# Down projections of two of three feed-forward parts: four feature tiles of a part by seven half-width products

## The chip, the cores and the metric

The kernel runs on one core of a Trainium2 chip. The engines are TensorE (PE, matrix products into PSUM), VectorE (DVE), ScalarE (ACT), GpSimd (POOL) and the queue that issues most transfers (SP). A transfer is issued by a queue and carried by the core's DMA engines. Each engine works through its own instructions in order and waits on semaphores for the others. The metric is the device time of one execution in microseconds (us); of the kernel before there are three runs. A profile is one further execution, recorded by the hardware.

## The reference

Two layers, 512 positions, 1024 features. Each layer has two feed-forward blocks with a mixer (a convolution and a differential attention) between them:

```python
def swiglu(h, w_gate, w_up, w_down):
    return (jax.nn.silu(h @ w_gate) * (h @ w_up)) @ w_down
...
    for l in range(DEPTH):
        x = x + 0.5 * swiglu(rms_norm(x, ffn1_norm[l]), ffn1_w_gate[l], ffn1_w_up[l], ffn1_w_down[l])
...
        x = x + jnp.concatenate([conv_out, diff_out], axis=-1) @ w_out[l]
        x = x + 0.5 * swiglu(rms_norm(x, ffn2_norm[l]), ffn2_w_gate[l], ffn2_w_up[l], ffn2_w_down[l])
```

The gated width is 2816, that is 22 feature tiles of 128; the output has 8 tiles of 128 features. All of it is float32 with a tight tolerance.

## The kernel before

**Products.** A float32 product is made of three matmuls on split operands: high weight by high activation, high by low, low by high (mm3, L174 to L178). A weight chunk of 128 x 1024 is loaded into a tile wraw; ACT copies it, rounded, into whi (L100), and DVE subtracts to get wlo (L101). These tiles come from rings shared by tag: five wraw, four each of whi and wlo, two half-size ones each (wraw2, whi2, wlo2). A slot is given out again when the last reader of its tile has been put in order. The order on every engine is made at build time by a scheduler; keep_in_program_order pins the first matmul of a group.

**The feed-forward block (ffn, L416).** x is kept as [128, 8, 512], features by positions. The 22 tiles are done in three parts of 5, 8 and 9 (PARTS). A part first computes its gated tiles (gate and up, silu, product), then projects them down into all eight outputs and adds them to x (L486). So there are 4 blocks x 3 parts.

**Seven products for gate and up (seven, L369).** From the sixth tile on, gate and up of a tile are the two rows of a two-by-two block product: the 1024 input features are two halves, the 512 positions two halves of 256. Seven products of half blocks (Strassen's scheme in Winograd's form) stand for eight. The weight sums are made in sums (L130 to L158) by POOL and by one accumulating DMA (L152), the activation sums in Halves. The products accumulate in two PSUM banks, a and d in one, b and c in the other; parts of them are copied to a tile keep by ACT (L391, L395, L400) in between. The seventh product and what follows it (rest, L406) are put off into the next tile, by way of late and finish, so that they stand behind the next tile's first two products.

**The down projection (L475 to L488)** is plain: for each output m, one bank, and for each of the part's tiles three full-width matmuls of 512 columns, 3 x 8 x 8 = 192 in part two and 216 in part three. gather loads eight blocks of 128 x 128 at a time, in pieces where they do not lie together. finish runs before it. In part three, after(m) hands x[m] to the next norm (Prep.tile, L260): ACT scales (L262) and squares (L271), DVE makes the low half (L263), POOL adds up the squares (L275).

**Banks.** Pairs of PSUM banks are taken in rotation from three tags (sc, po, mm) by a running number; two more tags, tp and y, have one bank each. Each block and each mixer starts the rotation at a number of its own.

Of the kernel before, what the change touches and what calls it, by code (L numbers as in the profile page):

```python
# [11 lines left out]
F32 = mybir.dt.float32  # L12
F32R = mybir.dt.float32r
# [5 lines left out]
P = 128  # L19
DEPTH = 2  # L20
# [23 lines left out]

PARTS = ((0, 5), (5, 8), (13, 9))
PLAIN = PARTS[0][1]
# [21 lines left out]
def trunk(ctx: ExitStack, tc: tile.TileContext, xt, par, lamv, relb, onehot,  # L68
# [12 lines left out]
    def f32(ap):  # L81
        return ap.bitcast(F32)
# [285 lines left out]

    def seven(halves, w, banks, fp, before, last):  # L369

# [25 lines left out]
        go(b, "g2", "b21")  # L396
        if not last:
            go(c, "all", "b22")
        go(a, "g1u2u1", "t2")
        S.activation(keep[:, 2], a, AF.Copy)  # L400
        if last:
            go(c, "all", "b22")
        V.tensor_tensor(two, two, g, op=ALU.add)
# [11 lines left out]

    def ffn(pr, gu, dn, after, lead=None, aside=None):  # L416
        with tc.tile_pool(name="ffn", bufs=1) as fp:
            r = halves = None
            for m0, many in PARTS:
                hh, held, late = [], [], []  # L420

                def gated(n, us):
                    hi = fp.tile([P, SEQ], F32R, tag=f"hh{n}", name="hh")
                    lo = fp.tile([P, SEQ], F32R, tag=f"hl{n}", name="hl")
                    S.activation(hi, us, AF.Copy)
                    V.tensor_tensor(lo, us, f32(hi), op=ALU.subtract)
                    hh.append((hi, lo))

                def finish():
                    if late:  # L430
                        n, rest = late.pop()
                        gated(n, rest())

                for mm in range(many):
# [3 lines left out]
                    if m >= PLAIN:  # L438
                        w = sums(gu[m, 0], gu[m, 1])
                        late.append((mm, seven(halves, w, pair_banks(m), fp, finish, mm == many - 1)))  # L440
                        continue
                    if lead and m < 2:
                        w = lead[m]
                    else:

                        w = [(by_halves if lead and m == 2 else chunk)(gu[m, 0]), chunk(gu[m, 1])]
                    held.append((mm, w, pair_banks(m)))
                    if m == 0:
# [21 lines left out]
                    if not halves:  # L470
                        halves = Halves(fp, pr, r)
                finish()
                if m0 == 0:
# [4 lines left out]
                for m in range(KT):  # L478

                    ps = bank(turn_tag(m0 + many + m // 2), "ps_d")  # L480
                    for kk in range(many):
                        b = m * many + kk
                        if b % 8 == 0:
                            w = gather(dn, blocks[b : b + 8])
                        mm3(ps, wpart(w, b % 8), hh[kk], kk == 0, kk == many - 1)
                    V.scalar_tensor_tensor(x[:, m, :], ps, 0.5, x[:, m, :], op0=ALU.mult, op1=ALU.add)  # L486
                    if m0 + many == FT:
                        after(m)  # L488


# [55 lines left out]

    def mixer(l, pr, after):
        with tc.tile_pool(name="mix", bufs=1) as mp, tc.tile_pool(name="mt", bufs=2) as mt:
            us = [None] * CT
            row = {}  # L550
            turn = iter(range(12))
            held = []
# [307 lines left out]
    def aside():  # L860
        make_scalars()
        make_bias()

    for l in range(DEPTH):
        nxt = {}
# [10 lines left out]

        ffn(pr, gu1[l], dn1[l], then(l, "mix_norm"), *((lead, aside) if l == 0 else ()))
        mixer(l, nxt["p"], then(l, "ffn2_norm"))
        ffn(nxt["p"], gu2[l], dn2[l], then(l + 1, "ffn1_norm") if l + 1 < DEPTH else last)
        pr = nxt["p"]  # L880
# [74 lines left out]
```

## Time and profile before

| What | us |
|---|---|
| Median of 3 runs | 1791.35 |
| Lowest and highest run | 1789.62, 1792.2 |
| Span of the profiled execution, first to last instruction | 1789.9 |
| PE busy in it | 1780.6 |
| DVE, ACT, POOL busy in it | 1192.0, 893.1, 668.9 |

The page's rows of engine totals give busy time, its share of the span and the number of instructions. The slices give tenths of busy time in 40 equal stretches, and PEclk the clock that TensorE was granted. The chain of waits follows the work that ended last back from the end; in order of time it gives start, length and what it was, merged where equal instructions follow each other. A window lists start and end, then busy us of PE, PEld (weight loads, beside PE), DVE, ACT and POOL with their instruction counts, the clock, and the share and rate of DMA. A row of a group gives line, engine, operation, output <- inputs, shapes, count, then busy us and mean ns of one, then the idle time of the engine just before them and what ended it. Rows of the timeline give start and length in us. Matmuls overlap, so that the distance of their starts, not their mean length, is what one costs.

### The profile page before, as it was taken

The page shows a single profiled execution, that of the slowest core. Times are in us where ns is not written, and L with a number is a line of the kernel's source. Part 1 is how long each engine was busy: PE and PEld are TensorE (multiplying, and loading weights), DVE is VectorE, ACT ScalarE, POOL GpSimd, SP SyncE. Part 2 cuts the span into 40 slices and gives each one's busy share as a digit, 9 for nine tenths or more (in the row PEclk, how much of TensorE's full clock was granted, in tenths as well). Part 3 has the DMA queues.
Part 4 walks back from the last instruction along what each step waited for, and adds up shares of the span by engine and source line. Part 5 has one row for each costly group of instructions (what it writes and reads, how often), then busy time and mean ns, then how long its engine had stood idle before and what let it go on. Part 6 is the DMA issues. An engine that isn't in the chain of part 4 may idle for free.

```text
span 1789.9 us, 28369 instructions
## 1 busy us (share of the span) xinstructions
PE 1780.6 (99%) x10861; PEld 1592.3 (89%) x10861; DVE 1192.0 (67%) x1833; ACT 893.1 (50%) x1487; POOL 668.9 (37%) x469
## 2 busy tenths in 40 slices
PE   9999999999999999999999999999999999999999
PEld 7899899888788899899888998998887988998997
DVE  6866477558858767477576655765788487664872
ACT  6455265445845455255433643644558354552651
POOL 2243242269863132232202412412798431422420
PEclk9999999999999999999999999999999999999999
DMA  7376466323122367367324655663230233664651
GB/s 247 106 181 179 112 175 179 114 98 94 36 83 88 90 165 191 104 171 195 101 93 101 169 167 124 174 180 118 71 117 25 71 107 97 167 172 112 168 163 59
DMA packets 111721, 231.24 MB, mean 129 GB/s; under 512 B 12151, under 2 KB 33414, under 8 KB 111584
## 3 DMA queue, kind: packets, MB, share of 16 engines
q1 hardware_dynamic: 91488, 191.93, 33.4%
q0 software_dynamic: 19808, 37.33, 12.7%
q8 instruction: 85, 1.39, 0.3%
q14 instruction: 52, 0.43, 0.1%
q10 hardware_dynamic: 288, 0.16, 0.0%
HBM read 227.26 MB, written 3.42 MB: 129 GB/s over the span
## 4 chain that ended last, share of the span: by engine, by line
PE 97%; DVE 2%; DMA 0%; issue 0%; SPq 0%; ACT 0%; DVEq 0%
PE ps_pair L386 38%; PE ps_d L177 9%; PE ps_d L174 9%; PE ps_d L178 9%; PE ps_pair L178 5%; PE ps_pair L177 5%; PE ps_pair L174 5%; PE ps_sc L726 2%; PE ps_pair L604 2%; PE ps_pair L602 2%; PE ps_pair L603 2%; PE ps_out L174 1%; PE ps_out L177 1%; PE ps_out L178 1%; PE ps_o L756 1%; DVE actl L263 1%
## 5 line engine op out<-in xcount | busy, mean ns | idle before, releaser
L100 ACT ACTIVATE whi<-wraw 128x512 fp32r<-128x512 f32 (+2 forms) x600 | 466.1, 801 | 617.9 <-PE ps_pair L386 225.1
L101 DVE TENSOR_TENSOR wlo<-wraw,whi 128x512 fp32r<-128x512 f32 (+2 forms) x557 | 514.4, 946 | 225.2 <-ACT whi L100 220.4
L386 PE MATMUL ps_pair<-acth,wlo 128*128 128x256 f32 x1088 | 307.9, 283 | 0.0
L386 PE MATMUL ps_pair<-actl,whi 128*128 128x256 f32 x1088 | 307.9, 283 | 0.0
L386 PE MATMUL ps_pair<-acth,whi 128*128 128x256 f32 x1088 | 307.9, 283 | 0.0
L177 PE MATMUL ps_d<-hl,whi 128*128 128x512 f32 x704 | 274.0, 389 | 0.0
L178 PE MATMUL ps_d<-hh,wlo 128*128 128x512 f32 x704 | 272.9, 389 | 0.0
L174 PE MATMUL ps_d<-hh,whi 128*128 128x512 f32 x704 | 269.1, 389 | 0.0
L152 POOL DMA_DIRECT2D wraw<-in_gu x68 | 82.0, 1206 | 407.3 <-DMA wraw<-in_gu 188.8
L386 PE MATMUL ps_pair<-th,wlo 128*128 128x256 f32 x816 | 230.9, 283 | 0.0
L386 PE MATMUL ps_pair<-tl,whi 128*128 128x256 f32 x816 | 230.8, 283 | 0.0
L386 PE MATMUL ps_pair<-th,whi 128*128 128x256 f32 x816 | 230.8, 283 | 0.0
L157 POOL TENSOR_TENSOR wraw<-wraw 128x512 f32<-128x512 f32 x68 | 106.6, 1568 | 328.0 <-DMA wraw<-in_gu 252.5
L386 PEld LDWEIGHTS ps_pair<-acth,whi 128*128 128x128 f32 x1088 | 208.9, 192 | 0.3
L386 PEld LDWEIGHTS ps_pair<-actl,whi 128*128 128x128 f32 x1088 | 208.9, 192 | 0.3
L386 PEld LDWEIGHTS ps_pair<-acth,wlo 128*128 128x128 f32 x1088 | 208.9, 192 | 0.0
L486 DVE SCALAR_TENSOR_TENSOR x<-ps_d,x 128x512 f32<-128x512 f32 x96 | 64.8, 689 | 180.4 <-PE ps_d L178 180.1
L177 PE MATMUL ps_pair<-actl,whi 128*128 128x512 f32 x448 | 174.6, 391 | 0.3 <-DVE actl L263 0.2
L174 PE MATMUL ps_pair<-acth,whi 128*128 128x512 f32 x448 | 173.9, 392 | 0.7 <-ACT whi L100 0.7
L178 PE MATMUL ps_pair<-acth,wlo 128*128 128x512 f32 x448 | 174.3, 391 | 0.0
L386 PEld LDWEIGHTS ps_pair<-tl,whi 128*128 128x128 f32 x816 | 156.5, 192 | 0.7
L386 PEld LDWEIGHTS ps_pair<-th,whi 128*128 128x128 f32 x816 | 156.5, 192 | 0.6
(171 smaller groups left out, 3264.9 us busy)
## 6 DMA issues: line engine op xcount, KB each, us to landing
wraw<-in_gu SPq DMA_DIRECT2D x208, 256.0 KB, 4.0
wraw<-in_gu SPq DMA_DIRECT2D x104, 512.0 KB, 3.7
wraw<-in_gu POOLq DMA_DIRECT2D x68, 512.0 KB, 5.7
wraw<-in_wqkv SPq DMA_DIRECT2D x24, 512.0 KB, 3.6
wraw<-in_dn SPq DMA_DIRECT2D x84, 128.0 KB, 3.0
wraw<-in_dn SPq DMA_DIRECT2D x32, 256.0 KB, 3.3
wraw<-in_wag SPq DMA_DIRECT2D x16, 512.0 KB, 3.6
wraw<-in_wout SPq DMA_DIRECT2D x16, 512.0 KB, 3.6
```

Of the source, the lines that this page charges most:

```text
L100: S.activation(hi, raw, AF.Copy)
L101: low = (eng or V).tensor_tensor(out=lo, in0=raw, in1=f32(hi), op=ALU.subtract)
L152: nc.gpsimd.dma_start(two.rearrange("p (b c) -> p b c", b=2), u[:, h[0]].unsqueeze(1).broadcast_to([P, 2, 512]), accum_op=ALU.add)
L157: G.tensor_tensor(more[:, h[0]], two[:, h[1]], whole[:, h[0]], op=ALU.add)
L174: first = T.matmul(ps, wh, xh, start=start, stop=False)
L177: T.matmul(ps, wh, xl, start=False, stop=False)
L178: T.matmul(ps, wl, xh, start=False, stop=stop)
L386: mm = T.matmul(ps, l, r, start=first and i == j == 0, stop=False, skip_group_check=True)
L486: V.scalar_tensor_tensor(x[:, m, :], ps, 0.5, x[:, m, :], op0=ALU.mult, op1=ALU.add)
L602: T.matmul(ps[n], xh[:, t], wh, start=k == 0, stop=False)
L603: T.matmul(ps[n], xh[:, t], wl, start=False, stop=False)
L604: T.matmul(ps[n], xl[:, t], wh, start=False, stop=k == KT - 1)
```

## The change

PARTS gains a third number, the pairs of feature tiles that are projected by seven products: none in part one, two in parts two and three. There, four feature tiles of the part are the inner dimension (two halves, each made of two tiles: the even and the odd ones), two outputs A = 2q and B = 2q + 1 are the rows, and the two halves of the positions the columns. The part's other four or five tiles are projected plainly into the same two outputs, A into the banks of b and c, B into a spare bank (tp or y).

- down_sums loads the blocks of A and B (g and u), and POOL makes four sums of 256 columns from them; what does not fit (the ninth tile) goes with one sum into a tile "two". Then all are split into high and low.
- seven_down issues the products, evicts parts of the banks into keep with ACT, adds these to x with POOL (lines 501 and 510 of the new file) and the banks to x with DVE (lines 513, 516, 520). Its last product, with the last update of x[B], is put off into the next pair, or into the next part's first tile, as rest.
- Gated.add takes the place of gated: beside the high and low of a gated tile it makes, for the first four tiles of a part, sums of their half blocks, on ACT and DVE, and stores them split.
- The running number of the banks is passed on (turn) through parts and into the mixer.
- seven loses its argument last, by which the last tile of a part ordered two products otherwise; the last gated tile of a part is finished within the first pair of the down projection.

```diff
@@ -42,7 +42,7 @@
 HS = SEQ // 2
-PARTS = ((0, 5), (5, 8), (13, 9))
+PARTS = ((0, 5, 0), (5, 8, 2), (13, 9, 2))
 PLAIN = PARTS[0][1]
 SPACE = 392
-    def seven(halves, w, banks, fp, before, last):
+    def seven(halves, w, banks, fp, before):
...
-        if not last:
-            go(c, "all", "b22")
+        go(c, "all", "b22")
         go(a, "g1u2u1", "t2")
         S.activation(keep[:, 2], a, AF.Copy)
-        if last:
-            go(c, "all", "b22")
         V.tensor_tensor(two, two, g, op=ALU.add)
         S.activation(g, two, AF.Silu)
...
-    def ffn(pr, gu, dn, after, lead=None, aside=None):
+    def down_sums(dn, m0, many, pairs, q):
+        def pull(raw, at, m, k, end):
+            while k < end:
+                half, f = divmod(m0 + k, HALF)
+                b, w = m * HALF + f, 1
+                while (b + w) % 8 and k + w < end and f + w < HALF:
+                    w += 1
+                c = b % 8
+                nc.sync.dma_start(raw[:, at : at + w * P], dn[half, b // 8][:, c * P : (c + w) * P])
+                at, k = at + w * P, k + w
+        A, B = 2 * q, 2 * q + 1
+        whole, over, J = min(many, 8), max(many - 8, 0), pairs * P
+        u, two, g = ring("wraw"), ring("wraw2", 512), ring("wraw")
+        pull(u, 0, B, 0, whole)
+        pull(g, 0, A, 0, whole)
+        pull(two, J, A, whole, many)
+        pull(two, J + over * P, B, whole, many)
+        more = ring("wraw")
+        def odd_even(t):
+            t = t[:, : 2 * J].rearrange("p (j e c) -> p e j c", e=2, c=P)
+            return t[:, 0], t[:, 1]
+        def row(t, n):
+            return t[:, n * J : (n + 1) * J].rearrange("p (j c) -> p j c", c=P)
+        (u1, u2), (g1, g2) = odd_even(u), odd_even(g)
+        G.tensor_tensor(row(two, 0), u1, u2, op=ALU.add)
+        G.tensor_tensor(u1, u1, g1, op=ALU.add)
+        G.tensor_tensor(row(more, 0), row(two, 0), g1, op=ALU.add)
+        G.tensor_tensor(row(more, 1), row(more, 0), g2, op=ALU.add)
+        def split(raw, tag, n, width):
+            hi, lo = ring("whi" + tag, n), ring("wlo" + tag, n)
+            parts_of(raw[:, :width], hi[:, :width], lo[:, :width])
+            return lambda at: (hi[:, at * P : (at + 1) * P], lo[:, at * P : (at + 1) * P])
+        two = split(two, "2", 512, J + 2 * over * P)
+        u = split(u, "", 1024, whole * P)
+        g = split(g, "", 1024, whole * P)
+        more = split(more, "", 1024, 2 * J)
+        return {
+            "u2u1": two,
+            "u2": lambda j: u(2 * j + 1),
+            "g1u1": lambda j: u(2 * j),
+            "g1": lambda j: g(2 * j),
+            "g2": lambda j: g(2 * j + 1),
+            "g1u2u1": more,
+            "all": lambda j: more(pairs + j),
+            "A": lambda k: g(k) if k < 8 else two(pairs + k - 8),
+            "B": lambda k: u(k) if k < 8 else two(pairs + over + k - 8),
+        }
+    def seven_down(q, w, h, banks, spare, fp, before, pairs, many, after, last):
+        A, B = 2 * q, 2 * q + 1
+        a, d = banks[0][:, :HS], banks[0][:, HS:]
+        b, c = banks[1][:, :HS], banks[1][:, HS:]
+        keep = fp.tile([P, 4, HS], F32, tag="gn", name="keep", bufs=2)
+        def by_two(t):
+            return t.rearrange("p (n c) -> p n c", n=2)
+        def go(ps, wt, xt, first=False):
+            for j in range(pairs):
+                (wh, wl), (xh, xl) = w[wt](j), h.get(xt, j)
+                for i, (l, r) in enumerate(((wh, xh), (wh, xl), (wl, xh))):
+                    mm = T.matmul(ps, l, r, start=first and i == j == 0, stop=False, skip_group_check=True)
+                    if i == j == 0:
+                        tc.keep_in_program_order(mm)
+        def plain(ps, wt, first=False):
+            for k in range(2 * pairs, many):
+                (wh, wl), (xh, xl) = w[wt](k), h.hh[k]
+                for i, (l, r) in enumerate(((wh, xh), (wh, xl), (wl, xh))):
+                    start = first and i == 0 and k == 2 * pairs
+                    mm = T.matmul(ps, l, r, start=start, stop=False, skip_group_check=True)
+                    if i == 0 and k == 2 * pairs:
+                        tc.keep_in_program_order(mm)
+        go(c, "u2u1", "t1", first=True)
+        S.activation(keep[:, 3], c, AF.Copy, scale=0.5)
+        go(d, "u2", "t4", first=True)
+        before()
+        go(a, "g1", "b11")
+        S.activation(keep[:, :2], by_two(banks[0]), AF.Copy, scale=0.5)
+        G.tensor_tensor(by_two(x[:, B, :]), by_two(x[:, B, :]), keep[:, 1::2], op=ALU.subtract)
+        go(b, "g2", "b21")
+        if last:
+            plain(banks[1], "A")
+        else:
+            go(c, "all", "b22")
+            plain(banks[1], "A")
+        go(a, "g1u2u1", "t2")
+        S.activation(keep[:, 2], a, AF.Copy, scale=0.5)
+        G.tensor_tensor(by_two(x[:, A, :]), by_two(x[:, A, :]), keep[:, 0::2], op=ALU.add)
+        if last:
+            go(c, "all", "b22")
+        V.scalar_tensor_tensor(x[:, A, :], banks[1], 0.5, x[:, A, :], op0=ALU.mult, op1=ALU.add)
+        after(A)
+        plain(spare, "B", first=True)
+        V.scalar_tensor_tensor(x[:, B, :], spare, 0.5, x[:, B, :], op0=ALU.mult, op1=ALU.add)
+        def rest():
+            go(a, "g1u1", "t3")
+            V.scalar_tensor_tensor(
+                by_two(x[:, B, :]), a.unsqueeze(1).broadcast_to([P, 2, HS]), -0.5, by_two(x[:, B, :]),
+                op0=ALU.mult, op1=ALU.add,
+            )
+            after(B)
+        return rest
+    class Gated:
+        STORE = (("ht", "ht", "rb"), ("s0", "s1", "s2"))
+        def __init__(self, fp, pairs):
+            self.fp, self.pairs = fp, pairs
+            self.hh, self.sums = [], []
+        def part(self, tag):
+            pool, bufs = (act, None) if tag == "rb" else (self.fp, 2 if tag == "ht" else None)
+            return pool.tile([P, SEQ], F32R, tag=tag, name="hs", **({"bufs": bufs} if bufs else {}))
+        def add(self, n, us):
+            a, b = slice(0, HS), slice(HS, SEQ)
+            paired = n < 2 * self.pairs
+            if paired and n % 2 == 0:
+                self.hold = self.fp.tile([P, SEQ], F32, tag=("hh8", "hl8")[n // 2 % 2], name="hold")
+                S.activation(self.hold, us, AF.Copy)
+                V.tensor_tensor(us[:, b], self.hold[:, a], self.hold[:, b], op=ALU.subtract)
+            hi = self.fp.tile([P, SEQ], F32R, tag=f"hh{n}", name="hh")
+            lo = self.fp.tile([P, SEQ], F32R, tag=f"hl{n}", name="hl")
+            S.activation(hi, us, AF.Copy)
+            V.tensor_tensor(lo, us, f32(hi), op=ALU.subtract)
+            self.hh.append((hi, lo))
+            if not paired or n % 2 == 0:
+                return
+            t = self.hold
+            V.tensor_tensor(t[:, b], us[:, b], t[:, b], op=ALU.subtract)
+            V.scalar_tensor_tensor(t[:, a], t[:, a], -1.0, t[:, b], op0=ALU.mult, op1=ALU.subtract)
+            V.scalar_tensor_tensor(us[:, a], us[:, a], -1.0, t[:, a], op0=ALU.mult, op1=ALU.subtract)
+            hi, lo, four = (self.part(tag) for tag in self.STORE[n // 2])
+            S.activation(hi, t, AF.Copy)
+            V.tensor_tensor(lo, t, f32(hi), op=ALU.subtract)
+            S.activation(four[:, a], us[:, a], AF.Copy)
+            V.tensor_tensor(four[:, b], us[:, a], f32(four[:, a]), op=ALU.subtract)
+            self.sums.append((hi, lo, four))
+        def get(self, name, j):
+            a, b = slice(0, HS), slice(HS, SEQ)
+            if name == "t4":
+                return self.sums[j][2][:, a], self.sums[j][2][:, b]
+            hi, lo = self.sums[j][:2] if name in ("t2", "t3") else self.hh[2 * j + (name[0] == "b" and name[1] == "2")]
+            c = a if name in ("b11", "b21", "t2") else b
+            return hi[:, c], lo[:, c]
+    def ffn(pr, gu, dn, after, turn, lead=None, aside=None):
         with tc.tile_pool(name="ffn", bufs=1) as fp:
             r = halves = None
-            for m0, many in PARTS:
-                hh, held, late = [], [], []
-                def gated(n, us):
-                    hi = fp.tile([P, SEQ], F32R, tag=f"hh{n}", name="hh")
-                    lo = fp.tile([P, SEQ], F32R, tag=f"hl{n}", name="hl")
-                    S.activation(hi, us, AF.Copy)
-                    V.tensor_tensor(lo, us, f32(hi), op=ALU.subtract)
-                    hh.append((hi, lo))
-                def finish():
-                    if late:
-                        n, rest = late.pop()
-                        gated(n, rest())
+            late = []
+            def finish():
+                if late:
+                    late.pop()()
+            for m0, many, pairs in PARTS:
+                held, h = [], Gated(fp, pairs)
+                gated, hh = h.add, h.hh
                 for mm in range(many):
                     m = m0 + mm
...
                         w = sums(gu[m, 0], gu[m, 1])
-                        late.append((mm, seven(halves, w, pair_banks(m), fp, finish, mm == many - 1)))
+                        rest = seven(halves, w, pair_banks(turn + mm), fp, finish)
+                        late.append(lambda n=mm, rest=rest, gated=gated: gated(n, rest()))
                         continue
                     if lead and m < 2:
                         w = lead[m]
                     else:
+                    held.append((mm, w, pair_banks(turn + mm)))
                     if m == 0:
                         continue
...
                         halves = Halves(fp, pr, r)
+                turn += many
+                if pairs:
+                    for q in range(KT // 2):
+                        w = down_sums(dn, m0, many, pairs, q)
+                        end = m0 + many == FT
+                        late.append(seven_down(
+                            q, w, h, pair_banks(turn), bank(("tp", "y")[q % 2], "ps_d"), fp, finish, pairs, many,
+                            after if end else lambda m: None, end and q == KT // 2 - 1,
+                        ))
+                        turn += 1
+                    continue
                 finish()
                 if m0 == 0:
...
-                    ps = bank(turn_tag(m0 + many + m // 2), "ps_d")
+                    ps = bank(turn_tag(turn + m // 2), "ps_d")
...
                         after(m)
+                turn += KT // 2
+            finish()
+        return turn
     skew = []
...
+    def mixer(l, pr, after, turn):
...
         make_scalars()
         make_bias()
+    turn = 0
     for l in range(DEPTH):
...
-        ffn(pr, gu1[l], dn1[l], then(l, "mix_norm"), *((lead, aside) if l == 0 else ()))
-        mixer(l, nxt["p"], then(l, "ffn2_norm"))
-        ffn(nxt["p"], gu2[l], dn2[l], then(l + 1, "ffn1_norm") if l + 1 < DEPTH else last)
+        turn = ffn(pr, gu1[l], dn1[l], then(l, "mix_norm"), turn, *((lead, aside) if l == 0 else ()))
+        mixer(l, nxt["p"], then(l, "ffn2_norm"), turn)
+        turn = ffn(nxt["p"], gu2[l], dn2[l], then(l + 1, "ffn1_norm") if l + 1 < DEPTH else last, 0)
         pr = nxt["p"]
```

More of the change, by code (lines that the diff above doesn't have):

```diff
@@ L446, in ffn @@
                         w = [(by_halves if lead and m == 2 else chunk)(gu[m, 0]), chunk(gu[m, 1])]
-                    held.append((mm, w, pair_banks(m)))
+                    held.append((mm, w, pair_banks(turn + mm)))
                     if m == 0:
@@ L544, in make_scalars @@
             G.tensor_scalar(pars[l][:, c : c + CT * TAPS], pars[l][:, c : c + CT * TAPS], 0.5, None, op0=ALU.mult)
-    def mixer(l, pr, after):
+    def mixer(l, pr, after, turn):
         with tc.tile_pool(name="mix", bufs=1) as mp, tc.tile_pool(name="mt", bufs=2) as mt:
@@ L550, in mixer @@
             row = {}
-            turn = iter(range(12))
+            turn = iter(range(turn, turn + 12))
             held = []
```

## The prediction

> **What bounds the kernel now.** I read the page's engine totals and slices first, then the chain of waits in order of time, then windows over one feed-forward block, then the groups by shape.
>
> ```profile
> PE 1780.6 (99%) x10861; PEld 1592.3 (89%) x10861; DVE 1192.0 (67%) x1833; ACT 893.1 (50%) x1487; POOL 668.9 (37%) x469
> ...
> PEclk9999999999999999999999999999999999999999
> ...
> PE 97%; DVE 2%; DMA 0%; issue 0%; SPq 0%; ACT 0%; DVEq 0%
> ```
>
> TensorE (PE) is busy 99% of the span, its clock is granted in full in every slice, and 97% of the chain that ended last is its own work. So the time is the number of matmuls times the distance between two starts, and the chain gives that distance:
>
> ```profile
> 77.00 1.13 PE ps_d L174 x5
> 184.87 0.68 PE ps_d L174 x3
> 531.14 0.12 PE ps_out L177
> 1103.44 86.39 PE ps_pair L386 x720
> ```
>
> A full-width matmul (512 columns) takes 0.68 / 3 = 0.227 us, a half-width one 86.39 / 720 = 0.120 us. The half costs 0.53 of the whole. (The groups' means, 389 and 283 ns, are longer because matmuls overlap.) Now the stages of one block:
>
> ```profile
> 170.00:215.00 45.00, 45.00 (x209) 37.64 (x208) 18.77 (x24) 10.50 (x14) 8.43 (x6) 1.00 0.44 111
> 215.00:305.00 90.00, 90.00 (x749) 89.83 (x748) 67.13 (x93) 54.95 (x95) 30.30 (x21) 1.00 0.66 177
> 305.00:360.00 55.00, 55.00 (x250) 45.77 (x249) 27.57 (x32) 22.18 (x29) 11.30 (x11) 1.00 0.42 127
> 400.00:600.00 200.00, 198.07 (x1040) 165.69 (x1039) 158.62 (x307) 116.28 (x217) 127.30 (x82) 1.00 0.27 79
> 1200.00:1400.00 200.00, 198.20 (x937) 162.39 (x936) 144.19 (x275) 116.02 (x216) 140.46 (x97) 0.99 0.27 82
> ```
>
> After the window come PE, PEld, DVE (VectorE), ACT (ScalarE) and POOL (GpSimd) busy. The first row is the second part's down projection, the second row the third part's gate and up tiles, the third row the third part's down projection. PE has no idle time in them. In the down stages DVE is half idle, ACT 60 to 77% and POOL some 80%: that is the room the new work goes into. In the gate/up stage DVE is at 67.13 of 90.
>
> **The change, part by part.** *The products.* A pair of outputs over four feature tiles was 2 x 4 x 3 = 24 full-width matmuls, 24 x 0.227 = 5.44 us. It becomes 7 products x 2 x 3 = 42 half-width ones, 42 x 0.120 = 5.04 us. The other four (part two) or five (part three) tiles stay as they are. There are 4 pairs, 2 parts and 4 blocks: 32 pairs, so 32 x 0.40 = 12.8 us less on the path that sets the end. The two forms of half-width matmul above run at one pace, so I take 0.120; bounds are half of 0.227, 0.113 (42 x 0.113 = 4.76, a gain of 21.8 us), and above, 0.1296, where the gain is nil and of which no row has a sign.
>
> [...]
>
> *Vector work per pair.* These rows price it:
>
> ```profile
> L101 DVE TENSOR_TENSOR wlo<-wraw,whi 128x1024 fp32r<-128x1024 f32 x203 | 261.2, 1292 | 56.0 <-ACT whi L100 51.5
> L101 DVE TENSOR_TENSOR wlo<-wraw,whi 128x512 fp32r<-128x512 f32 x346 | 249.7, 754 | 168.0 <-ACT whi L100 167.7
> L486 DVE SCALAR_TENSOR_TENSOR x<-ps_d,x 128x512 f32<-128x512 f32 x96 | 64.8, 689 | 180.4 <-PE ps_d L178 180.1
> L408 DVE TENSOR_TENSOR ps_pair<-ps_pair,keep 128x256 f32<-128x256 f32 x68 | 29.3, 431 | 48.2 <-PE ps_pair L386 48.2
> L158 POOL TENSOR_TENSOR wraw<-wraw 128x512 f32<-128x512 f32 x68 | 126.4, 1859 | 5.3
> L275 POOL TENSOR_TENSOR ssum<-ssum,sq 128x512 f32<-128x512 f32 x35 | 56.2, 1605 | 199.1 <-ACT sq L271 193.1 <-DVE wlo L101 5.5
> L100 ACT ACTIVATE whi<-wraw 128x1024 fp32r<-128x1024 f32 x247 | 259.5, 1058 | 367.2 <-PE ps_d L177 171.2 <-PE ps_pair L177 84.5 <-PE ps_pair L386 55.9
> L100 ACT ACTIVATE whi<-wraw 128x512 fp32r<-128x512 f32 x346 | 203.8, 626 | 248.7 <-PE ps_pair L386 169.2 <-PE ps_d L177 45.0 <-issue 18.5
> L395 ACT ACTIVATE keep<-ps_pair 128x512 f32<-128x512 f32 x68 | 40.6, 597 | 37.0 <-PE ps_pair L386 37.0
> L391 ACT ACTIVATE keep<-ps_pair 128x256 f32<-128x256 f32 x68 | 26.2, 385 | 12.6 <-PE ps_pair L386 4.8
> L262 ACT ACTIVATE acth<-x,par 128x512 fp32r<-128x512 f32 x48 | 34.1, 717 | 55.4 <-DVE x L486 30.9 <-DVE x L848 23.1 <-DMA par<-in_par 0.8
> L271 ACT ACTIVATE sq<-x 128x512 f32<-128x512 f32 x42 | 25.8, 619 | 2.8 <-DVE x L848 1.7 <-DVE ssum L275 1.1
> ```
>
> A pair of part two lasts 5.04 + 24 x 0.227 = 10.48 us on PE, of part three 5.04 + 30 x 0.227 = 11.84. In part three ACT does splits of 1024, 1024, 512 and 512 columns (2 x 1.06 + 2 x 0.63) and evictions of 512, 256 and 256 (0.60 + 2 x 0.39): 4.7 us. DVE does the low halves (2 x 1.29 + 2 x 0.75) and three updates of x (2.07): 6.2 us. POOL does four sums of 256 columns and two updates of x; at 1.29 us per 512 columns uncontended (row below) that is 4 x 0.65 + 2 x 1.29 = 5.2. All fit, so these cost nothing while PE's own queue covers them. The steady cover for weights: the next pair's g needs a slot of the high-half ring that this pair's plain products of A give back. From there PE has 0.72 + 2.72 + 3 x 0.72 = 5.6 us of work in part two before it needs g; ACT and DVE take 1.06 + 1.29 = 2.4. If that cover were gone, each pair would wait up to 2.4 us.
>
> *The put-off product.* The seventh product of a pair is issued in the next pair, or in the next part's first tile, as in gate and up. At a block's end it comes last: then DVE's update, gain, square and POOL's sum, 0.69 + 0.72 + 0.62 + 1.61 = 3.6 us, before PE wants the sum of squares, which in the built order is 30 full-width matmuls, 6.8 us, later: nothing. The program's very end keeps its one update of x and one DMA.
>
> *The half-block sums of the gated tiles* (Gated.add) add two copies of 512 columns and one of 256 on ACT (1.6 us per pair of tiles), and on DVE 0.43 in the even tile and 4 x 0.43 + 0.69 = 2.4 in the odd one. A gate/up tile is 84 x 0.120 = 10.08 us, of which DVE uses 7.5 by the window; the odd tile rises to 9.9, still below 10.08. ACT's splits there wait mostly for PE to give back slots (169.2 of 248.7 us in the row above), so weights run ahead: nothing; if DVE's other waits eat the rest, 0 to 1 us per part.
>
> *DMA and transitions.* The same bytes of weights come in, in a few more pieces on SP's queue. The first half-width tile of part three now prepares its weights while two updates of x wait on POOL behind its accumulating DMA:
>
> ```profile
> wraw<-in_dn SPq DMA_DIRECT2D x32, 256.0 KB, 3.3
> wraw<-in_gu POOLq DMA_DIRECT2D x68, 512.0 KB, 5.7
> ```
>
> The update of x (L510 of the new file) waits about 6 us there, DVE behind it; the tile's own splits still come some 1.5 us before PE wants them. Into part two, ACT's copy of the last gated tile stands behind a split that waits for a POOL sum, which waits for a 3.3 us load: following the queues, its low half is ready about 0.2 us after PE asks for it. Bounds 0 and 1; I take 0.2 x 4 = 0.8 us.
>
> *The wait that I expect to show* is in part three of the three blocks whose down projection feeds the next norm (all but the last). There the first product of b in a pair waits for ACT's eviction of c (same PSUM bank), and in the built order that eviction stands behind the norm's work on the pair before. From the moment A's plain products have read g: split of g 1.06, split of the sums once a is done (at 1.40) 0.63, eviction of a 0.39, POOL's update 1.29, DVE's update 0.69, gain 0.72, square 0.62, a split of 0.63, eviction of c 0.39: 6.8 us, and some 0.05 for each of eight changes of engine: 7.2. PE gets there after 0.68 + 0.72 + 3.40 + 4 x 0.72 = 7.7. So 0.5 us of slack, if POOL is free and uncontended. It is not always:
>
> ```profile
> 229.43 1.23 DVE L101 TENSOR_TENSOR wlo<-wraw,whi 128x1024 fp32r<-128x1024 f32 x1
> 248.95 1.28 POOL L157 TENSOR_TENSOR wraw<-wraw 128x512 f32<-128x512 f32 x1 [5.23 <-DMA wraw<-in_gu]
> 249.59 1.73 DVE L101 TENSOR_TENSOR wlo<-wraw,whi 128x1024 fp32r<-128x1024 f32 x1
> 250.31 2.17 POOL L158 TENSOR_TENSOR wraw<-wraw 128x512 f32<-128x512 f32 x1
> 332.23 0.75 DVE L263 SCALAR_TENSOR_TENSOR actl<-x,par,acth 128x512 fp32r<-128x512 f32 x1 [0.79 <-ACT acth L262]
> ```
>
> Where a DVE subtraction of two SBUF operands meets a POOL sum, both stretch: 1.23 to 1.73 and 1.28 to 2.17, the sum of both being what one after the other would take. With POOL's update at its mean under contention (L158, 1.86) and now and then a sum or a square's sum ahead of it, the wait per pair lies between nothing and 0.57 + 0.9 + 1.86 - 0.5 = 2.8 us. I take 0.5, near the lower end because POOL is idle for a third of a pair (7.8 of 11.84, worked out below). Three pairs in each of three blocks: 9 x 0.5 = 4.5 us.
>
> *The mixers* get other PSUM banks (the rotation now runs on) and another order of instructions. PE idles 1.9 and 1.8 us in their windows: 2 us each way for either, 0 taken.
>
> *The sum:* -12.8 + 0.8 + 4.5 = -7.5 us. The profiled execution has a span of 1789.9, 1.45 below the median 1791.35; the difference goes onto the median: 1783.9. Ends of the known terms: all waits covered, 1778.6; waits at 1.4 us in the nine pairs, 1791.9.
>
> **Rivals.** *All covered.* POOL and ACT keep ahead and only the products count: 1791.35 - 12.8 = 1778.5. For it: PE's lack of idle time in the same seven-product scheme of gate and up. Against: the slack of 0.5 us.
>
> *No change: POOL and DVE exclude each other.* In part three with the norm, DVE's two-operand work is 2 x 1.23 + 2 x 0.69 + 2 x 0.75 = 5.3 us a pair, POOL's 5.2 + 2 x 1.29 = 7.8; one after the other 13.1, against 11.84 on PE. At 1.3 us over in nine pairs the gain shrinks by 11.7: 1791.35 - 12.8 + 0.8 + 11.7 = 1791.0. For it the stretched rows; against, that the last squares' sums may trail into the next stage.
>
> [...]
>
> *Slower: the eviction behind the norm.* POOL's update comes late by its whole queue in every one of the nine pairs, 9 x 2.8 = 25.2 us: 1791.35 - 12.8 + 0.8 + 25.2 = 1804.6. It decides from 12.0 / 9 = 1.3 us per pair. For it: ACT, DVE and POOL each stand in line for the next. Against: half the queue ahead of the update is done before.
>
> *It does not do what it says:* no; PE's matmuls rise by 32 x 18 = 576.
>
> **How the numbers follow.** Forecast 0.50 (its own spread 1780 to 1787.5), all covered 0.20, no change 0.14, slower 0.11, better than all covered 0.05 (pace or mixers). A change under 0.2% (3.6 us) can't be told from none here: above 1787.8 counts as the same, above 1794.9 as slower. Faster: 0.48 + 0.20 + 0.05 + some of the third, 0.76; same 0.13; slower 0.11. The range 1777 to 1792 leaves out the slower case and the far end of the pace.
>
> **What would show it.** Right: 11437 matmuls; pairs of 10.48 us in part two; PE waiting some tenths at a product of b in part three, released by ACT's eviction of c, in three blocks but not the last; POOL sums above 1.29. Wrong: waits in part two's steady pairs; PE waiting for weights in the first tile of part three; a pace other than 0.120; the mixers longer by over 2 us.

## The result and the profile after

The changed kernel takes 1798.99 us (median of 4 runs, 1796.62 to 1802.17) against 1790.51 us before (4 runs). The ratio worked out from the runs is 1.0049, 95% interval 1.0035 to 1.0063 (here and below it is not exactly the quotient of the two medians). It is slower by 8.5 us, where 7.5 us less was forecast. The profiled execution, the slowest of the four, has a span of 1800.2 us, 10.3 us above the span of before.

The page after, its totals of busy time and the clock that TensorE was granted in 40 slices:

```profile
span 1800.2 us, 30317 instructions
...
PE 1776.3 (99%) x11437; PEld 1609.4 (89%) x11437; DVE 1343.9 (75%) x2021; ACT 977.6 (54%) x1691; POOL 884.8 (49%) x661
...
PEclk9999999999999999999999999999999999999999
```

The 576 additional matmuls are there, and PE is still busy 99%. That share hides the loss: 1800.2 - 1776.3 = 23.9 us without work, against 1789.9 - 1780.6 = 9.3 before. (Busy time fell by 4.3 us and not by 12.8. It is not the clock: each of the two executions has one stretch of 3.4 us at half clock, shown below; in a slice of 45 us it does not show. Presumably it is the tails of matmuls, which overlap with the next one unless it comes late: a half-width matmul lasts 0.28 us by the view, at a distance of 0.12. No run tests this.)

First the products. The chain that ended last, after (start, length, what, and the count of matmuls), with a pair of part two from its product of a to that of the next pair, and the same in part three:

```profile
1636.12 4.31 PE ps_pair L482 x36
1640.43 2.75 PE ps_pair L491 x12
1643.18 0.71 PE ps_pair L482 x6
1643.89 2.75 PE ps_d L491 x12
1646.64 4.31 PE ps_pair L482 x36
...
1759.78 4.31 PE ps_pair L482 x36
...
1771.66 4.31 PE ps_pair L482 x36
```

1646.64 - 1636.12 = 10.52 and 1771.66 - 1759.78 = 11.88 us, for 10.48 and 11.84 forecast, and 4.31 / 36 = 0.120 us for a half-width matmul. So the products are nearly as cheap as the prediction says: 12.8 us leave TensorE's path, less 32 x 0.04 = 1.3 us by which the pairs are longer than forecast. What came in their place stands in TensorE's waits. Before, this was the whole list (producer, then total us, times, longest), all of it in the mixers and at the starts of blocks:

```profile
PE ps_o L756 <- DVE actl L786: 1.7, 2, 0.8
PE ps_sc L726 <- DVE e L740: 1.4, 4, 0.5
PE ps_idle L198 <- DVE relb L495: 1.0, 1, 1.0
PE ps_pair L174 <- ACT whi L100: 0.7, 2, 0.5
PE ps_sc L726 <- DVE mn L730: 0.5, 2, 0.3
PE ps_pair L177 <- DVE actl L263: 0.2, 1, 0.2
```

And after:

```profile
PE ps_pair L386 <- ACT keep L395: 3.7, 4, 1.2
PE ps_pair L386 <- DVE wlo L101: 1.9, 4, 1.0
PE ps_pair L491 <- ACT hh L549: 1.8, 1, 1.8
PE ps_v L799 <- ACT qz L815: 1.8, 1, 1.8
PE ps_pair L482 <- ACT keep L496: 1.8, 4, 0.8
PE ps_pair L491 <- DVE hl L550: 1.5, 4, 0.6
PE ps_sc L893 <- DVE e L907: 1.4, 2, 0.7
PE ps_pair L386 <- ACT keep L399: 1.1, 1, 1.1
...
PE ps_o L950 <- DVE ov L938: 0.8, 1, 0.8
```

Only the fifth row is the wait that was forecast. The view counts from a matmul's modelled end. Taking the starts of all matmuls from TensorE's timeline instead, and the distance of each to the next less its usual pace, the change lost 23 us more than the kernel before, in these places:

| place | us | where in the span a wait begins |
|---|---|---|
| gated tiles just ahead of the down projections of parts two and three | 5.2 | 158, 294, 706, 843, 1056, 1192 |
| first pair of part two | 4.7 | 177, 726, 1075, 1620 |
| first gated tiles of part three | 4.3 | 214, 233 to 238, 1112, 1122 |
| products of b (forecast 4.5) | 3.4 | 322, 335, 871, 884, 1220, 1233 |
| first mixer (198.2 us long, 194.7 before; some 1.7 of it a stretch at half clock) | 3.5 | 448 to 555 |
| gaps too small to name, the pairs' own 1.3 us among them | 2 | |

The first two places have one cause, as the order of ScalarE's queue shows here and e4 tests below. ScalarE's timeline after, on the way into part two of the second block and into part three of it (start, length, line, and in brackets the idle time ahead and what ended it):

```profile
725.37 1.36 ACT L100 ACTIVATE whi<-wraw 128x256 fp32r<-128x256 f32 x2 [3.05 <-POOL wraw L442]
726.64 0.58 ACT L500 ACTIVATE keep<-ps_pair 128x512 f32<-128x512 f32 x1
727.36 0.60 ACT L549 ACTIVATE hh<-ps_pair 128x512 fp32r<-128x512 f32 x1
...
843.44 0.63 ACT L100 ACTIVATE whi<-wraw 128x512 fp32r<-128x512 f32 x1 [3.41 <-POOL wraw L442]
843.97 0.58 ACT L395 ACTIVATE keep<-ps_pair 128x512 f32<-128x512 f32 x1
```

GpSimd's and TensorE's timelines beside them:

```profile
724.60 0.74 POOL L442 TENSOR_TENSOR wraw<-wraw 128x256 f32<-128x256 f32 x1 [5.80 <-DMA wraw<-in_dn]
842.68 0.72 POOL L442 TENSOR_TENSOR wraw<-wraw 128x256 f32<-128x256 f32 x1
```

```profile
728.01 0.49 PE L491 MATMUL ps_pair<-hh,whi 128*128 128x512 f32 x1 [1.82 <-ACT hh L549]
844.61 0.38 PE L386 MATMUL ps_pair<-th,whi 128*128 128x256 f32 x1 [1.24 <-ACT keep L395]
```

ScalarE is idle for 3 us, not overloaded. At the head of its queue stands a weight split of a coming down pair (L100 on the sum of u1 and u2), which waits for GpSimd's sum L442, which waits for a load or for GpSimd's other sums. Behind the split stand the evictions of the gated tile that is still running: L395, and the copy L549 that the plain products read. TensorE needs these first, and waits. The rows show the evictions start within 0.1 us of the end of the splits ahead of them: L500, which stands ahead of L549, at 726.64 (the two splits end at 725.37 + 1.36 = 726.73), and L395 at 843.97 (843.44 + 0.63 = 844.07).

### The profile page after: what moved, and what is told of

It reads as the page before. It is cut to its first block, busy times and chain, and to the rows that moved or that the text cites. A ratio compares the mean times of both kernels' runs of the same rounds, so it can differ in the third digit from the quotient of the medians.

```text
span 1800.2 us, 30317 instructions
## 1 busy us (share of the span) xinstructions
PE 1776.3 (99%) x11437; PEld 1609.4 (89%) x11437; DVE 1343.9 (75%) x2021; ACT 977.6 (54%) x1691; POOL 884.8 (49%) x661
## 5 line engine op out<-in xcount | busy, mean ns | idle before, releaser
L100 ACT ACTIVATE whi<-wraw 128x512 fp32r<-128x512 f32 (+3 forms) x660 | 496.0, 777 | 498.1 <-PE ps_pair L386 135.5
L101 DVE TENSOR_TENSOR wlo<-wraw,whi 128x512 fp32r<-128x512 f32 (+2 forms) x617 | 602.7, 1000 | 179.2 <-ACT whi L100 174.2
L157 POOL TENSOR_TENSOR wraw<-wraw 128x512 f32<-128x512 f32 x68 | 104.7, 1540 | 309.0 <-DMA wraw<-in_gu 205.5
L386 PEld LDWEIGHTS ps_pair<-th,wlo 128*128 128x128 f32 x816 | 156.6, 192 | 0.0
L101 POOL TENSOR_TENSOR wlo<-wraw,whi 128x1024 fp32r<-128x1024 f32 x44 | 105.5, 2402 | 37.3 <-ACT whi L100 37.3
L861 DVE SCALAR_TENSOR_TENSOR ps_y<-u,par,ps_y 128x512 f32<-128x512 f32 x156 | 117.6, 754 | 3.7
L158 POOL TENSOR_TENSOR wraw<-wraw 128x512 f32<-128x512 f32 x68 | 116.1, 1707 | 5.3
```

The lines of the kernel that those rows point to most:

```text
L100: S.activation(hi, raw, AF.Copy)
L101: low = (eng or V).tensor_tensor(out=lo, in0=raw, in1=f32(hi), op=ALU.subtract)
L157: G.tensor_tensor(more[:, h[0]], two[:, h[1]], whole[:, h[0]], op=ALU.add)
L158: G.tensor_tensor(more[:, h[1]], more[:, h[0]], whole[:, h[1]], op=ALU.add)
L386: mm = T.matmul(ps, l, r, start=first and i == j == 0, stop=False, skip_group_check=True)
L861: V.scalar_tensor_tensor(ys[c] if t == PAD and not n else y, us[c][:, t : t + SEQ], pars[l][:, wc + t : wc + t + 1], y, op0=ALU.mult, op1= ...
```

## Experiments

Each experiment's time is a median against runs of the kernel before on the same chip; e1 to e4 share one set of those (1789.93 us), e5 to e8 one (1790.17), e9 to e11 one (1790.02), and e12 has its own (1790.28). The brackets give 95% intervals. Line numbers are the same in all changed kernels.

### One part at a time (e1, e2, e3)

```diff
-PARTS = ((0, 5, 0), (5, 8, 2), (13, 9, 2))
+PARTS = ((0, 5, 0), (5, 8, 0), (13, 9, 0))   # e1
+PARTS = ((0, 5, 0), (5, 8, 2), (13, 9, 0))   # e2
+PARTS = ((0, 5, 0), (5, 8, 0), (13, 9, 2))   # e3
```

> The changed kernel with no pairs in any part (third numbers of PARTS all 0): plain down projections, but the new put-off step through Gated.add and the running bank number remain. Theory (the time went into waits where the down stages begin and end, behind weight splits that wait for POOL's sums): those waits are gone, 10.4 us of gaps on TensorE as in the kernel before, 1790.5 us, ratio 1.000. Rival (the running bank number costs about 3.7 us in the first mixer): 1794, ratio 1.002, with the same gaps at 493 to 506 us as in the changed kernel.

> Seven products in part two alone. Products: 16 pairs x 0.40 = 6.4 us less. Theory: part two's own waits stay, some 6.4 us in its last gated tiles and at its first pair and 4.3 us in the first tiles of part three: 1790.5 - 6.4 + 10.7 = 1794.8, ratio 1.0024. Rival (VectorE and GpSimd exclude each other and fall behind in part three's norm pairs): that place is plain here, so 1784 to 1786. If the mixer's gaps come from the bank numbers, 3.7 more in either.

> Seven products in part three alone. Products: 6.4 us less. Theory: waits of 3.7 us in the last gated tiles of part three and 3.4 us at the products of b: 1790.5 - 6.4 + 7.1 = 1791.2, ratio 1.0004. Rival (exclusion in the norm pairs): all of the changed kernel's 23 us of waits hang on this part, 1798 or more.

Measured: e1 1795.98 us, ratio 1.0030 (1.0019 to 1.0042); e2 1793.78, 1.0023 (1.0013 to 1.0034); e3 1797.48, 1.0038 (1.0026 to 1.0051).

e1 decides for the rival, and by more than it forecast: without one of the new products the kernel loses 6.0 us. Its feed-forward blocks have hardly any waits; its first mixer is 198.4 us long. That leaves e2 6.4 us of products and some 4 us of waits (1796.0 - 6.4 + 4 = 1793.6; its time came close to the theory's, for another reason), and e3 6.4 us of products and some 8 us of waits (by its starts 10 us, of which the products of b 2.4). e3's time lies next to its rival's 1798, 6 us above its theory, but 6.0 us are e1's loss, which e3 has too; and that the trouble sits in the norm's pairs falls with the waits: in e3 TensorE's largest is the gated tile's eviction:

```profile
PE ps_pair L386 <- ACT keep L395: 5.6, 4, 2.3
```

The two parts do not add up: by e2 and e3 the change would take 1796.0 - 2.2 + 1.5 = 1795.3 us, and it takes 1799.0.

### The split behind the eviction (e4)

```diff
-        S.activation(keep[:, :2], banks[0].rearrange("p (n c) -> p n c", n=2), AF.Copy)
+        mark["ad"] = S.activation(keep[:, :2], banks[0].rearrange("p (n c) -> p n c", n=2), AF.Copy).ins
...
-            S.activation(hi, us, AF.Copy)
+            mark["hh"] = S.activation(hi, us, AF.Copy).ins
...
-        two = split(two, "2", 512, J + 2 * over * P)
+        with tc.issue_after(mark["ad"] if q == 0 else mark["hh"]):
+            two = split(two, "2", 512, J + 2 * over * P)
```

> The changed kernel, where ScalarE's split of the first pair's u2-u1 sum is queued behind the eviction of a and d of the last gated tile, and the second pair's behind the copy of the last gated tile. No work is added or taken. Theory (the split stands in ScalarE's queue ahead of evictions that TensorE waits for): 3.7 us in part three's and 4 to 6 us in part two's last gated tiles and first pairs go, 1799.0 - 8 = 1791, ratio about 1.000. Rival (the engines' work itself is too much, so that it is late wherever it stands): the waits move to the first product of the pair, 1797 to 1800.

Measured: 1790.98 us, ratio 1.0002 (0.9993 to 1.0011), against 1.0049 for the change: 8 us back, as the theory said, with the same work. The first edit is at L395, the second at L549, the third in down_sums. ScalarE's timeline in e4, at the place of the 3.41 us above:

```profile
843.70 1.06 ACT L100 ACTIVATE whi<-wraw 128x1024 fp32r<-128x1024 f32 x1 [1.11 <-PE ps_pair L386]
845.21 0.60 ACT L395 ACTIVATE keep<-ps_pair 128x512 f32<-128x512 f32 x1 [0.45 <-PE ps_pair L386]
```

L395 now waits for TensorE, and not TensorE for L395. The waits at L491 are gone from e4's view too.

### The bank numbers (e5, e6, e9)

The change counts PSUM bank numbers on through a block and hands the count to the mixer, which used to start at 0. A feed-forward block uses 34 numbers and the tags go round by three, so the two mixers start at 34 and 68, that is at 1 and 2.

```diff
-        mixer(l, nxt["p"], then(l, "ffn2_norm"), turn)
+        mixer(l, nxt["p"], then(l, "ffn2_norm"), 2)         # e5 on e1, e6 on e4
```
```diff
-                turn += many
+                turn += many + (m0 > 0)                     # e9 on e1: 36 numbers a block
```

> No seven products in any down projection (as in e1), and both mixers start their rotation of banks at number 2, where the changed kernel's second mixer starts, instead of 1 and 2. Theory (the bank number with which the first mixer starts costs 3.7 us there, and a drop of the granted clock in it the rest): first mixer back to about 195 us from 198.4, 1790.5 to 1791.5, ratio 1.000 to 1.001. Rival (the put-off step and the new order in the feed-forward blocks cost it): 1795 to 1796 as e1.

> e4's order of the two weight splits and both mixers started at bank number 2. Theory (the two costs are separate and add): 1791.0 - 4 = 1787, ratio 0.998. Rival (mixer time does not hang on the banks): 1791.

> No seven products in any down projection (as in e1), with the running bank number moved on by one at the end of the gated tiles of parts two and three, so that every block uses 36 numbers and both mixers start at bank number 0 as in the kernel before. Theory (all of e1's loss is the bank numbers with which the mixers start, 1 and 2): 1790 to 1791, ratio 1.000. Rival (the put-off step or the order in the feed-forward blocks costs the 4.3 us that were left in e5): 1794, ratio 1.002.

Measured: e5 1794.46 us, ratio 1.0022 (1.0012 to 1.0031); e6 1786.32, 0.9974 (0.9963 to 0.9984), as its theory said; e9 1790.22, 1.0004 (0.9995 to 1.0013). Mixer lengths, from the start of the last down matmul ahead to that of the last output matmul:

| start number, first and second mixer | kernel | first | second |
|---|---|---|---|
| 0, 0 | before | 194.7 | 196.2 |
| 1, 2 | e1 | 198.4 | 196.3 |
| 2, 2 | e5 | 196.2 | 196.3 |
| 0, 0 | e9 | 194.6 | 194.9 |

(The second mixer of before holds a drop of the clock worth 1.7 us, below.) e5 fell between its two theories: starting at 2 is better than at 1, and still worse than at 0. e9 settles it: with both mixers at 0 the kernel without products is as fast as before, so the put-off step through Gated.add costs nothing when no half-block sums are made, and the bank numbers cost 1795.98 - 1790.22 = 5.8 us. A wait that shows it, in e1's second mixer (start 2) and gone in e9:

```profile
PE ps_v L799 <- ACT qz L815: 1.8, 1, 1.8
```

The value projection always takes the "mm" banks. With start 2 the last query and key pair but one sits in them, and its transposed result has first to be evicted by ScalarE (L815). With start 0 the "mm" pair is an earlier one. For start 1, no single row carries the 3.7 us; that it is the number is shown, the steps between are not. Some 1.7 us of it are a stretch at half clock (last section): the profiled executions of the changed kernel, e1 and e4, all with start 1, have a granted clock of 0.83 from 500 to 510 us; before, with start 0, has 1.00 there, and e5, e6, e7, e9 and e11, with start 0 or 2, have a mean of 1.0 over the whole execution.

### The norm's work, and room for the sums (e7, e8)

```diff
-        after(A)                                            # e7, on e6, in seven_down()
+        after(A) if q == KT // 2 - 1 else None
...
-            after(B)                                        # in rest(); mark["c"] is L496
+            with tc.issue_after(mark["c"]):
+                [after(k) for k in (A, B)[q == KT // 2 - 1 :]]
```
```diff
-        more = ring("wraw")                                 # e8, on e6, in down_sums()
+        more = fp.tile([P, SEQ], F32, tag=("hh8", "hl8")[q % 2], name="more") if many == 8 else ring("wraw")
...
```

> e6, and in the pairs whose outputs feed a norm the norm's activations on the output pair are queued on ScalarE behind the next pair's eviction of c. Theory of the prediction (the eviction of c stands behind the norm's work, which stands behind VectorE's and GpSimd's updates of x): the waits at the products of b, 3.2 us in e4's profile, are gone, 3 us less than e6. Rival (GpSimd and VectorE exclude each other, so the updates themselves are late): the waits go to the sums of squares or stay, same as e6 within 1 us.

> e6, and in part two the tile of the weights' last two sums is taken from buffers that are idle then, so a pair holds two of the five raw-weight buffers and not three. Same work. Theory (after part two the weights of the next gated tiles load late because raw buffers come free late): the waits at 213 and 233 to 238 us of the block (2.5 us in e4) and at the same place of the third block go, 2 to 3 us less than e6. Rival (VectorE and ScalarE have too much to do in the gated tiles, with the half-block sums on top): same as e6 within 1 us.

Measured: e7 1783.69 us, ratio 0.9959 (0.9947 to 0.9972), 2.6 us below e6; e8 1785.19, 0.9970 (0.9958 to 0.9981), 1.1 us below e6. Both intervals overlap with e6's, e7's less, so the traces decide. In e7's view of waits L496 no longer occurs and nothing took its place: the prediction's mechanism for the products of b holds, and the rival's forecast, that the waits stay or move, did not come. How much of the norm's lateness is GpSimd's updates stretched beside VectorE is not shown. ScalarE's timeline in the changed kernel shows the queue that e7 turns round, the norm's two activations and a split ahead of the eviction:

```profile
870.54 0.72 ACT L262 ACTIVATE acth<-x,par 128x512 fp32r<-128x512 f32 x1 [4.09 <-DVE x L513]
871.17 0.62 ACT L271 ACTIVATE ssum<-x 128x512 f32<-128x512 f32 x1
871.69 0.61 ACT L100 ACTIVATE whi<-wraw 128x512 fp32r<-128x512 f32 x1
872.21 0.36 ACT L496 ACTIVATE keep<-ps_pair 128x256 f32<-128x256 f32 x1
```

In e8 the 1.83 us that e6's starts show at 232 to 237 us are gone (at the same place of the third block e6 has none left); in the second mixer, which the edit does not touch, the profiled execution has 1.6 us more, with a stretch at half clock that e6's has not (mean clock 0.999 in e8, 1.0 in e6). That weights are late at this place shows in ScalarE's timeline of the changed kernel, where a split of the next gated tile's weights waits 2.15 us for their load (2.10 us in e6; in e8 no split there waits for a load):

```profile
232.36 0.63 ACT L100 ACTIVATE whi<-wraw 128x512 fp32r<-128x512 f32 x1 [2.15 <-DMA wraw<-in_gu]
```

So the theory is right about the place, and its 2 to 3 us are not shown.

### Together (e10, e11, e12)

e10 is the changed kernel with e9's line alone; e11 has all four edits (e4, e7, e8, e9); e12 has those of e4 and e9.

> The changed kernel with only that shift of the bank number; the splits, the norm's order and the raw buffers stay as in the change. Theory (bank numbers and waits at the down stages' ends add): 1799.0 - 5.5 = 1793.5, ratio about 1.002. Rival (the mixers' gaps come from the new down stages, not from the numbers): 1799.

> The changed kernel with all four edits: the shift of the bank number, the two splits queued behind the evictions (e4), the norm's activations behind the eviction of c (e7), the sums' own room in part two (e8). Theory (nothing but TensorE's matmuls is left of the change): the prediction's case that all is covered, 1790.2 - 12.8 = 1777.4, and 1779 to 1780 with what the trace of e7 leaves; ratio 0.993 to 0.994. Rival (a pace above 0.120 us or engines too full): not below e7, 1783.

> e10's shift of the bank number together with e4's order of the two weight splits; the norm's order and the raw buffers stay as in the change. e10 gave back only 1.4 us where 5.5 were forecast: its mixers are as short as before, but TensorE waits 7.7 us for ScalarE's evictions in gated tiles and 2.6 us at the second product of the first pairs. Theory (these are the same splits ahead of the evictions, which meet the shifted banks one product earlier): with the splits behind, 6 to 10 us go, 1790.2 - 12.8 + 3 (products of b) + 2 (first tiles of part three) = 1782 to 1784, ratio 0.9955 to 0.9965. Rival (the shifted banks are themselves in the way at the first pairs): the 2.6 us stay, 1786 to 1788.

Measured: e10 1797.64 us, ratio 1.0037 (1.0025 to 1.0050); e11 1779.36, 0.9942 (0.9929 to 0.9954); e12 1780.94, 0.9949 (0.9935 to 0.9962).

e10 missed its forecast: its mixers are 194.6 us each, yet it gained 1.4 us and not 5.5. Its waits say why:

```profile
PE ps_pair L386 <- ACT keep L395: 4.6, 4, 2.3
PE ps_pair L386 <- ACT keep L399: 3.1, 3, 1.1
PE ps_pair L482 <- DVE hl L550: 2.6, 5, 0.8
```

The shifted count lets a first pair take the banks of the tile before the last one, whose copies are just then late, so the same late queue is met earlier and costs more (the third row is new). That the banks are the step between is argued from the code and this row, not tested alone. With the two splits moved, e12, all three rows are gone and 16.7 us go with them, more than the 6 to 10 expected: the two edits do not add, each is worth little or much by the other. e11 is faster than both kernels, 10.7 us below before, as its theory said; the edits of e7 and e8 bring only 1.6 us on top of e12, with overlapping intervals. TensorE's waits in e11 are those of e9, the kernel without products: beside three rows of the mixers, there are 1.4 us in the program's first 10 us and 0.2 us where the second feed-forward block starts:

```profile
PE ps_idle L198 <- DVE relb L662: 1.0, 1, 1.0
...
PE ps_pair L174 <- ACT whi L100: 0.4, 1, 0.4
PE ps_pair L177 <- DVE actl L263: 0.2, 1, 0.2
```

## Why the prediction was wrong, by its own steps

Two of the four signs of being wrong that the prediction named came: TensorE waiting for weights in the first tiles of part three, and a mixer longer by over 2 us.

*The products, -12.8 us:* right but for 1.3 us. The pace is 0.120 us, the pairs last 10.52 and 11.88 us, and e11 is 10.9 us faster than e9, which has the same bank numbers and no products.

*Steady pairs cost nothing:* right in part two, no wait there. In part three the pairs wait only at b.

*The product of b, 4.5 us:* mechanism and place right (three blocks, not the last, released by L496); 3.4 us in the profile, 2.6 us by e7. What this step costs hangs on the others: in e12, without e7's edit, the products of b wait 0.65 us in all by the starts. The slower rival put 25.2 us on this same step; the kernel was slower, but not by it.

*DMA and transitions, 0.8 us:* the main failure. The prediction did follow the split that waits for GpSimd's sum on the way into part two, and took 0.2 us for each entry from load times and queue order, with 1 us as the bound. Measured were 4.7 us at the four first pairs, one alone 3.0. And it looked only at the copy L549: such a split also stands a tile earlier, ahead of the eviction L395 of a gated tile, for another 5.2 us. So this term was 9.9 us by the starts and not 0.8; moving two splits back took 8 us off.

*The half-block sums, 0 to 1 us per part:* 4.3 us in the first gated tiles of part three. With the splits moved 2.5 were left in e4 and 1.8 in e6, and e8 removed these by giving part two's sums other buffers, with VectorE's work unchanged: late weights set them (the 2.15 us above), not VectorE's 9.9 of 10.08 us. (They are gone in e12 too, which has not got e8's edit, so room is one cure and not the only one.) That "weights run ahead" was read from a kernel whose down projections take two raw buffers for two outputs; the new pairs take three and give them back after a sum on GpSimd.

*The mixers, 2 us each way, 0 taken:* the second failure, 5.8 us by e1 and e9. The prediction had named the new bank numbers and the new order, and had no price for them; it took the middle of a bound that was too narrow for the first mixer (3.5 us longer). It also read the clock as granted in full: the 0.99 in its last window row is before's stretch at half clock.

*No change by exclusion:* GpSimd's updates of x do rise, from the 1.29 us taken to 1.57 and 1.63 us on average, as in these rows of the groups after, but no wait of TensorE's was traced to it.

```profile
L501 POOL TENSOR_TENSOR x<-x,keep 128x512 f32<-128x512 f32 x32 | 52.3, 1633 | 18.9 <-ACT keep L500 18.8
L510 POOL TENSOR_TENSOR x<-x,keep 128x512 f32<-128x512 f32 x32 | 50.1, 1567 | 18.2 <-ACT keep L509 18.2
```

The sum as measured, in medians: -12.8 for the products, +5.8 for the bank numbers (by e1 and e9, without products; in the changed kernel e10's shift alone gave back only 1.4), and the rest of the +8.5, so 15.5 us, for the pairs' own 1.3 and the waits around the down stages (17.6 by the starts in the one profiled execution).

## What to carry to other kernels

When a change gives an engine work that waits for a longer chain (load, sum, split), look at what stands behind that work in the engine's queue, at the place where stages meet and not in the steady state; an engine that is 54% busy can still be the one that is late. A counter that is passed on to later stages is part of a change: try it with the rest switched off, as in e1. Two faults that met in one queue did not add here, so a mend that brings little alone (e10) is to be tried again with the other one in.

## What the runs showed of the hardware

TensorE's clock fell to half in a mixer without any long pause. Windows of the changed kernel (after the window: its length, PE, PEld, DVE, ACT and POOL busy, then the granted clock), and of the kernel before in its second mixer:

```profile
498.84:502.25 3.41, 1.90 (x11) 1.18 (x10) 3.29 (x12) 3.41 (x13) 2.87 (x4) 1.00 0.01 2
502.25:505.67 3.42, 3.04 (x10) 2.66 (x11) 3.42 (x12) 3.33 (x11) 1.09 (x2) 0.50 0.00 0
```

```profile
1384.02:1387.43 3.41, 1.82 (x11) 1.18 (x10) 3.41 (x16) 3.41 (x11) 3.09 (x5) 1.00 0.00 0
1387.40:1390.90 3.50, 3.50 (x17) 3.40 (x17) 2.93 (x11) 3.00 (x11) 2.88 (x3) 0.51 0.00 0
```

Both times 3.41 us with PE 1.8 to 1.9 us busy come first, and then some 3.4 us at half clock (0.50 and 0.51), which costs some 1.7 us. In the first of these TensorE idles in short pieces, the longest 0.8 us (L950 above).

What sets off the drop is not shown, and PE's busy time alone does not decide. In the changed kernel's second mixer PE is busy for less, with one pause of 1.8 us (L799 above), and the full clock goes on:

```profile
1345.35:1348.76 3.41, 1.64 (x12) 1.24 (x10) 1.20 (x2) 2.89 (x6) 3.41 (x3) 1.00 0.00 0
1348.76:1352.18 3.42, 3.38 (x15) 2.80 (x16) 2.77 (x4) 2.28 (x4) 3.42 (x3) 1.00 0.53 158
```

The first mixer of before has the same thin place as its second one (1.80 us busy from 496.00 to 499.40) and keeps its clock: 1.00 there and in the 3.4 us behind it.
